# Indexer queries of whole token tiles loaded one tile ahead in a fused two-block transformer kernel

## The chip, the cores and the metric

The kernel runs on one NeuronCore of a Trainium2 chip. That core has five engines with an instruction queue each: TensorE (PE, matrix products), VectorE (DVE), ScalarE (ACT), GpSimd (POOL) and SyncE (SP, which here does nothing but issue DMAs). Every queue is worked off in order: an instruction that waits holds back all that stand behind it. Sixteen DMA engines move data between the chip's main memory and the on-chip memory. The metric is the device time of one execution in microseconds; the kernel before takes 2626.92 us (median of three runs, 2626.12 to 2632.38).

## The reference

Two transformer blocks run one after the other on 1024 tokens of width 1024, in float32. The first (dilated attention, spatial gating, feed-forward) is not touched. The second is, cut to what matters:

```python
def _dsa_attention(q, k, v, q_idx, k_idx, w_idx):     # per block of 128 queries:
    logits = einsum('bthd,bsd->bths', qib, k_idx) * IDX_DIM ** -0.5    # 8 indexer heads of 64
    score = einsum('bth,bths->bts', wb, relu(logits))
    score = where(causal, score, -inf)
    _, sel = lax.top_k(score, 256)                     # keys that this query may look at
    ...                                                # attention of 8 heads over those keys

def second_block(...):
    q, k, v, qi, ki, wi, cu = split(h @ w_in)          # qi: indexer queries, cu: convolution input
    attn_out = _dsa_attention(rope(q), rope(k), v, rope(qi), rope(ki), wi)
    conv_out = _conformer_conv(cu, ...)                # gated; 31 taps per channel; norm; silu
    x = x + gt1 * (concat(attn_out, conv_out) @ w_out)
    x = x + gt2 * (square(relu(norm(x) @ w_up)) @ w_down)
```

## The kernel before, in words

**Tiling.** The 1024 tokens are two halves of 512, and eight tiles of 128 (tiles 0 to 3 in half 0, 4 to 7 in half 1). Every float32 matrix operand of weight is split in a high and a low part, and a product is three matmuls (lines 147, 148, 149), so the feed-forward networks fill most of TensorE's time.

**What runs beside what.** Attention and convolution of block 2 are a chain of dependent steps with little TensorE work. `flow` weaves such a side chain into a feed-forward network: half 0 of block 2 beside the second half of block 1's network (tiles `fa`, `fa1o`), half 1 beside the first half of block 2's own network (`fb`, `fb0o`). `flow` goes by an estimated clock: every `yield e, d` of a side chain says that it spent `e` us of TensorE and wants to be called again `d` us later (`d` from the table `LT`); between the calls feed-forward steps are written out. A scheduler then orders each engine's instructions by priority and by its own estimate of when buffers come free, so that the order on an engine isn't the order of the source.

**The side chain of one half** (`block2_side`, L1330): `b2_glu` writes the convolution's gated input to main memory (`glu_d`); `b2_conv` (L1066) runs as a chain of its own and, for each of four channel groups j, loads `glu` (L1071, one buffer) and does 31 steps on DVE, of which the first (L1073) waits for that load and the others are L1075; `b2_proj` forms the queries, turns them to one row per feature (L1007 to L1015) and stores them in main memory (`qiT_d` for the indexer, `qT_d` for the attention). Then come the scores: for each tile, `b2_scores` (L1128) loads the indexer queries of four heads (`load_q`, L1109), multiplies them by the keys (`scores_mm`, L1125, tiles `ip`), and per head does a relu on ACT (L1143, tile `ir`, in one of the five buffers of tag `PT`) and a multiply-add on DVE (L1146 and L1148, tile `sc`). `b2_topk` searches each query's 256th score bit by bit on DVE (L1162) and ACT (L1183) and ends in a mask (L1220). `b2_attn` (L1222) loads the attention queries with the same `load_q` (tile `qt`), forms scores (L1125, `sp`), masks and exponentiates (L1240, L1243), transposes (L1268), splits the result (L1270, L1271: `PT`, `PL`) and multiplies by the values (`o`).

**The loads in question.** `load_q` fills a tile `q` of 128 x 2 x 512 in two DMAs of 256 KB (z = 0, 1): 64 rows of main memory, read twice to fill 128 partitions. The tag `q` has two buffers (`QB2`), shared by indexer and attention queries, so the loads of a group of four heads wait until the group two before it has been multiplied. Scores of tiles 0 and 1 need no queries, which leaves 8 such DMAs in half 0 and 16 in half 1, each named `qi` in the trace, beside 32 named `qt`.

Of the kernel before, what the change touches and what calls it, by code (L numbers as in the profile page):

```python
# [10 lines left out]
F32R = mybir.dt.float32r  # L11
# [17 lines left out]
LT = {'att0': 11.236,  # L29
 'bit': 2.0,  # L30
 'conv': 12.0,
 'cvn': 3.332,
 'ex': 18.659,
 'fin': 4.025,
 'mods': 5.62,
 'n4': 6.0,
 'norm': 7.406,
 'qk': 12.0,
 'rope': 3.856,
 'ropeT': 2.236,  # L40
# [8 lines left out]
QB2 = 2  # L49
# [68 lines left out]
def tile_hybrid_two_blocks(ctx, tc, A, out, dbg=None, stop=None):  # L118
# [60 lines left out]
    def split_in(src, hi, lo, name):  # L179

        for t in range(2):
            sl = slice(2 * t, 2 * t + 2)
            raw = ring.tile([128, 2, 512], F32, tag="raw", name=f"{name}_r{t}", bufs=RBUF)
            for k in range(2):
                SP.dma_start(raw[:, k, :], src[2 * t + k])
            split_into(raw, hi[:, sl], lo[:, sl])
# [161 lines left out]
    def T_tiles(n, name):  # L348
        return [tp.tile([128, 4, 512], F32R, tag="T", name=f"{name}{i}") for i in range(n)]
# [82 lines left out]
    for td, o, n in ((tabA_d, 0, LA), (tabB_d, LA, LB)):  # L432
        p = psd.tile([NH, n], F32, tag="s", name=f"tabp{o}")
# [14 lines left out]
    for g2 in range(2):  # L448
        p = psd.tile([128, 4, 128], F32, tag="s", name=f"swp{g2}")
# [279 lines left out]
    for half in range(2):  # L729
# [3 lines left out]
        for f in range(4):  # L733
            p = psd.tile([128, 512], F32, tag="s", name=f"sgp{half}{f}")
# [11 lines left out]
    xu = ctx.enter_context(tc.tile_pool(name="xu", bufs=1, reuse_waits="tile"))  # L746
# [100 lines left out]
    for half in range(2):  # L847
# [3 lines left out]
        for q in range(4):  # L851
            i = 4 * half + q
# [90 lines left out]
    p = psd.tile([128, 4, 32], F32, tag="s", name="cwp")  # L943
# [18 lines left out]
    qiT_d = [dram.tile([2, 128, 512], F32, name=f"qiT_d{i}") for i in range(NT)]  # L962
# [143 lines left out]
            DVE.tensor_tensor(cl[:, j, :], ys[:, j, :], ch[:, j, :].bitcast(F32), op=ALU.subtract)  # L1106
        return ch, cl

    def load_q(d, g, name):  # L1109

        q = xu.tile([128, 2, 512], F32R, tag="q", name=name, bufs=QB2)
        for z in range(2):
            SP.dma_start(q[:, z, :].bitcast(F32), bass.AP(tensor=d.tensor, offset=d.offset + z * 128 * 512 + g * 64 * 512,
                                             ap=[[0, 2], [512, 64], [1, 512]]))
        return q

    def spans(n):

        m = n // -(-n // 512)
        return [(c0, m) for c0 in range(0, n, m)]  # L1120

    def scores_mm(q, j, g, c0, m, name):
        p = psd.tile([128, m], F32, tag="s", name=name)
        for z in range(2):
            PE.matmul(p, q[:, z, 128 * j:128 * j + 128], kT[:, g, c0:c0 + m], start=z == 0, stop=z == 1)  # L1125
        return p

    def b2_scores(i, sc):  # L1128

        n = 128 * (i + 1)  # L1130
        dg = slice(n - 128, n)
        if i < 2:
            if i:
                POOL.memset(sc[:, 0:128], 0.0)
            DVE.tensor_scalar(sc[:, dg], tri, -NEG, None, op0=ALU.mult)
            return
        for h in range(8):
            if h % 4 == 0:
                q = load_q(qiT_d[i], h // 4, f"qi{i}{h}")
            for c0, m in spans(n):  # L1140
                p = scores_mm(q, h % 4, 2, c0, m, f"ip{i}{h}")
                t = xu.tile([128, 512], F32, tag="PT", name=f"ir{i}{h}", bufs=PTB)
                ACT.activation(t[:, :m], p, AF.Relu)  # L1143
                o = sc[:, c0:c0 + m]
                if h == 0:
                    DVE.tensor_scalar(o, t[:, :m], wis[:, i, 0:1], None, op0=ALU.mult)  # L1146
                else:
                    DVE.scalar_tensor_tensor(o, t[:, :m], wis[:, i, h:h + 1], o, op0=ALU.mult, op1=ALU.add)  # L1148
            if h % 2 or n > 512:
                e = n / 512 * (1 if n > 512 else 2)  # L1150
                yield 2 * MM * e, LT["score"] * e / 2
        DVE.scalar_tensor_tensor(sc[:, dg], tri, -1.0e38, sc[:, dg], op0=ALU.mult, op1=ALU.add)
# [160 lines left out]
    def end_ffn1(half, acc):  # L1313

        gpf = grow(A["g_post_ffn"][0], f"gpf{half}")
        hi, lo = T_tiles(2, f"h3h{half}"), T_tiles(2, f"h3l{half}")
        for q in range(4):
            i = 4 * half + q
            a = acc[q]
            x = xtile(f"xf{i}")  # L1320
            SP.dma_start(x, x1_d[i])
            r = rms_r(a, 1e-6, f"po{i}")
            DVE.scalar_tensor_tensor(a, a, r, gpf, op0=ALU.mult, op1=ALU.mult)
            DVE.tensor_tensor(x, x, a, op=ALU.add)
            SP.dma_start(x2_d[i], x)
            if "x2" in dbg:
                SP.dma_start(dbg["x2"][128 * i:128 * i + 128], x)
            yield from norm_T(a, x, rms_r(x, 1e-6, f"n3{i}"), hi, lo, q, 0, f"h3{i}")
        return hi, lo

    def block2_side(half, acc):
        Th, Tl = yield from end_ffn1(half, acc)
        yield from b2_glu(half, Th, Tl)
        conv = yield Spawn(b2_conv(half), CP)
        qs = yield from b2_proj(half, Th, Tl)
        tiles = [4 * half + q for q in range(4)]
        sc = {}

        def scores(p):
            t = tp.tile([128, 2, S], F32, tag="T", name=f"sc{p[0]}")  # L1340
            for e, i in enumerate(p):
                sc[i] = t[:, e, :]
                yield from b2_scores(i, sc[i])

        def rows_of(i):
            return sc[i][:, 0:128 * (i + 1)]

        jk = xu.tile([128, S], BF16, tag="jk", name=f"jk{half}", bufs=1)

        def keep(i):  # L1350
            return b2_topk(f"{i}", jk, [rows_of(i)], [rows_of(i + 1)])

        busy[0] += 1
        if half:
            yield from scores(tiles[0:2])
            ks = [(yield Spawn(keep(4)))]
            yield from scores(tiles[2:4])
            ks.append((yield Spawn(keep(6))))
            busy[0] -= 1
            yield Join(qs)  # L1360
            for u in range(2):
                yield Join(ks[u])
                yield 0, LT["att0"]
                yield from b2_attn([(i, sc[i]) for i in tiles[2 * u:2 * u + 2]])
        else:
            yield from scores(tiles[2:4])
            busy[0] -= 1
            k_ = yield Spawn(keep(2))
            yield from scores(tiles[0:2])
            yield Join(qs)  # L1370
            yield from b2_attn([(i, sc[i]) for i in tiles[0:2]])
            yield Join(k_)
            yield 0, LT["att0"]
            yield from b2_attn([(i, sc[i]) for i in tiles[2:4]])
        cv = yield Join(conv)
        mT = [(None, None), cv]

        def mixed(k, q):
            if k < 4 and mT[0][0] is None:
                mT[0] = (T_tiles(1, f"ath{half}")[0], T_tiles(1, f"atl{half}")[0])  # L1380
                split_in(at2_d[half], *mT[0], f"at2{half}")
            return [t[:, k % 4, 128 * q:128 * q + 128] for t in mT[k // 4]]

        w = A["w_out_2"][0]
        gt1 = grow(gate_d[0], f"gt1{half}")
        ss = [small.tile([128, 2], F32, tag="ss4", name=f"ss4{half}{q}", bufs=4) for q in range(4)]
        for c in range(2):
            cs = slice(512 * c, 512 * c + 512)

            def ev(q, p):  # L1390
                i = 4 * half + q
                x = xu.tile([128, 512], F32, tag="P", name=f"x3p{i}{c}", bufs=PB)
                SP.dma_start(x, x2_d[i][:, cs])
                t = xu.tile([128, 512], F32, tag="PT", name=f"x3t{i}{c}", bufs=PTB)
                DVE.tensor_tensor(t, p, gt1[:, cs], op=ALU.mult)
                DVE.tensor_tensor(x, x, t, op=ALU.add)
                SP.dma_start(x3_d[i][:, cs], x)
                ACT.activation(junk[:, 0:512], x, AF.Square, accum_out=ss[q][:, c:c + 1])
            yield Job(tok_steps(mixed, w, [(512 * c, 512)], 2, f"w2{half}{c}", ev, first=4, two=4))
        hi, lo = T_tiles(2, f"h4h{half}"), T_tiles(2, f"h4l{half}")  # L1400
        yield 0, LT["n4"]
        for q in range(4):
            i = 4 * half + q
            s1 = small.tile([128, 1], F32, tag="ss", name=f"ss5{i}")
            DVE.tensor_tensor(s1, ss[q][:, 0:1], ss[q][:, 1:2], op=ALU.add)
            r = rsqrt_mean(s1, D, 1e-6, f"n4{i}")
            x = xtile(f"x4{i}")
            SP.dma_start(x, x3_d[i])
            yield from norm_T(x, x, r, hi, lo, q, 1, f"h4{i}")
        return hi, lo  # L1410
# [65 lines left out]
    acc, _ = flow(ffn1(0), mods())  # L1476
# [29 lines left out]
```

## Time and profile before

| | |
|---|---|
| median of 3 runs | 2626.92 us |
| profiled execution | 2627.51 us, of which the span of recorded instructions is 2625.7 us |
| mean granted TensorE clock | 0.968 of full speed |
| PE / DVE / ACT / POOL busy | 93% / 57% / 46% / 9% of the span |
| indexer products (L1125, `ip`) | 160 matmuls, 63.6 us busy, 51.2 us of PE idle before them |

The span runs from the first recorded instruction to the last; 1.8 us of the profiled execution lie outside it. A row's idle time is what the engine spent without work just before it, put down to what came last.

### The profile page before, as it was taken

The page shows a single profiled execution, that of the slowest core. Times are in us where ns is not written, and L with a number is a line of the kernel's source. Part 1 is how long each engine was busy: PE and PEld are TensorE (multiplying, and loading weights), DVE is VectorE, ACT ScalarE, POOL GpSimd, SP SyncE. Part 2 cuts the span into 40 slices and gives each one's busy share as a digit, 9 for nine tenths or more (in the row PEclk, how much of TensorE's full clock was granted, in tenths as well). Part 3 has the DMA queues.
Part 4 walks back from the last instruction along what each step waited for, and adds up shares of the span by engine and source line. Part 5 has one row for each costly group of instructions (what it writes and reads, how often), then busy time and mean ns, then how long its engine had stood idle before and what let it go on. Part 6 is the DMA issues. An engine that isn't in the chain of part 4 may idle for free.

```text
span 2625.7 us, 32724 instructions
## 1 busy us (share of the span) xinstructions
PE 2448.8 (93%) x12024; PEld 2001.5 (76%) x12024; DVE 1497.4 (57%) x2755; ACT 1216.5 (46%) x2160; POOL 242.4 (9%) x356
## 2 busy tenths in 40 slices
PE   8999999999999999679999999878889999799997
PEld 8867777778788787457888878667678887688886
DVE  3356444476654468367443257799997554533436
ACT  4345554453333443255545373366664443533332
POOL 1034311100000000000000000123200000100002
PEclk9999999999999999689999999989899999899999
DMA  6412114589976666345558657522222225633332
GB/s 180 121 44 64 42 37 118 172 298 320 295 257 194 223 206 220 125 132 179 167 164 271 195 161 212 168 90 80 65 84 80 86 69 160 229 96 96 97 96 72
DMA packets 330784, 391.64 MB, mean 149 GB/s; under 512 B 42273, under 2 KB 227889, under 8 KB 330624
## 3 DMA queue, kind: packets, MB, share of 16 engines
q1 hardware_dynamic: 327216, 385.11, 47.1%
q10 hardware_dynamic: 3408, 4.46, 0.5%
q8 instruction: 94, 1.54, 0.2%
q14 instruction: 66, 0.54, 0.1%
HBM read 312.44 MB, written 80.73 MB: 150 GB/s over the span
## 4 chain that ended last, share of the span: by engine, by line
PE 58%; DVE 14%; DMA 12%; issue 10%; ACT 3%; POOL 2%; SPq 1%; POOLq 0%; DVEq 0%; ACTq 0%
DVE y L1075 4%; DMA qi<-qiT_d 4%; PE fa_p L147 3%; PE fa_p L149 3%; PE fa_p L148 3%; PE fb_p L147 3%; PE fb_p L148 3%; PE fb_p L149 3%; PE oT L685 2%; PE fa0o_p L148 2%; PE fa0o_p L149 2%; PE fa0o_p L147 2%; PE fb1o_p L148 2%; PE fb1o_p L149 2%; PE fb1o_p L147 2%
## 5 line engine op out<-in xcount | busy, mean ns | idle before, releaser
L147 PE MATMUL fb_p<-h4h,fb_w_h 128*128 128x512 f32 x512 | 205.9, 403 | 12.6 <-ACT h4h L841 8.2
L147 PE MATMUL fa_p<-h2h,fa_w_h 128*128 128x512 f32 x512 | 205.1, 401 | 0.7 <-DVE fa_a L795 0.7
L149 PE MATMUL fa_p<-h2h,fa_w_l 128*128 128x512 f32 x512 | 203.9, 398 | 1.8 <-DMA fa_w_l<-fa_w_d 1.8
L148 PE MATMUL fa_p<-h2l,fa_w_h 128*128 128x512 f32 x512 | 204.8, 400 | 0.0
L148 PE MATMUL fb_p<-h4l,fb_w_h 128*128 128x512 f32 x512 | 204.5, 400 | 0.0
L149 PE MATMUL fb_p<-h4h,fb_w_l 128*128 128x512 f32 x512 | 203.5, 398 | 0.0
L1075 DVE SCALAR_TENSOR_TENSOR y<-glu,cw,y 128x512 f32<-128x512 f32 x240 | 193.8, 807 | 4.5
L176 ACT CAST fb_w_h<-fb_w_r 128x1024 fp32r<-128x1024 f32 x64 | 67.2, 1050 | 154.2 <-PE fb1o_p L149 74.1
L147 PEld LDWEIGHTS fb_p<-h4h,fb_w_h 128*128 128x128 f32 x512 | 97.9, 191 | 33.9 <-ACT h4h L841 8.6
L1183 ACT ACTIVATE junk<-sc,cand 128x768 bf16<-128x768 f32 (+2 forms) x93 | 86.8, 934 | 66.7 <-DVE cand L1181 64.7
L147 PEld LDWEIGHTS fa_p<-h2h,fa_w_h 128*128 128x128 f32 x512 | 97.1, 190 | 23.1 <-issue 1.1
L149 PEld LDWEIGHTS fa_p<-h2h,fa_w_l 128*128 128x128 f32 x512 | 96.9, 189 | 22.3 <-DMA fa_w_l<-fa_w_d 2.2
L148 PEld LDWEIGHTS fb_p<-h4l,fb_w_h 128*128 128x128 f32 x512 | 97.7, 191 | 21.0 <-DVE h4l L842 0.4
L148 PEld LDWEIGHTS fa_p<-h2l,fa_w_h 128*128 128x128 f32 x512 | 97.1, 190 | 21.4 <-issue 0.9
L149 PEld LDWEIGHTS fb_p<-h4h,fb_w_l 128*128 128x128 f32 x512 | 97.5, 191 | 20.1
L177 DVE TENSOR_TENSOR fb_w_l<-fb_w_r,fb_w_h 128x1024 fp32r<-128x1024 f32 x53 | 64.8, 1223 | 83.6 <-ACT fb_w_h L176 78.9
L1125 PE MATMUL ip<-kT,qi 128*128 128x384 f32 (+3 forms) x160 | 63.6, 429 | 51.2 <-DMA qi<-qiT_d 39.5
L1271 DVE TENSOR_TENSOR PL<-pt,PT 128x512 fp32r<-128x512 f32 (+1 forms) x80 | 50.6, 635 | 70.5 <-ACT PT L1270 70.5
L176 ACT CAST fa_w_h<-fa_w_r 128x1024 fp32r<-128x1024 f32 x32 | 33.7, 1054 | 118.4 <-PE fa0o_p L149 77.8
L1125 PEld LDWEIGHTS ip<-kT,qi 128*128 128x128 f32 x160 | 35.2, 226 | 65.2 <-DMA qi<-qiT_d 39.0
L1162 DVE TENSOR_SCALAR_CACHE_REDUCE jk<-sc,cand 128x640 bf16<-128x640 f32 (+2 forms) x93 | 81.4, 876 | 1.9
L177 DVE TENSOR_TENSOR fb1o_w_l<-fb1o_w_r,fb1o_w_h 128x1024 fp32r<-128x1024 f32 x28 | 34.3, 1225 | 83.9 <-ACT fb1o_w_h L176 83.9
(1511 smaller groups left out, 7103.1 us busy)
## 6 DMA issues: line engine op xcount, KB each, us to landing
fa_w_r<-in_w_ff_dram SPq DMA_DIRECT2D x64, 512.0 KB
fb_w_r<-in_w_up_dram SPq DMA_DIRECT2D x64, 512.0 KB
ada_w<-in_w_ada_dram SPq DMA_DIRECT2D x48, 512.0 KB
fa_w_d<-fa_w_l SPq DMA_DIRECT2D x32, 512.0 KB
fa0o_w_r<-in_w_ff_dram SPq DMA_DIRECT2D x32, 512.0 KB
fa0o_w_d<-fa0o_w_l SPq DMA_DIRECT2D x32, 512.0 KB
fa_w_l<-fa_w_d SPq DMA_DIRECT2D x32, 512.0 KB
fa1o_w_r<-in_w_ff_dram SPq DMA_DIRECT2D x32, 512.0 KB
```

The costliest lines, as they stand in the source:

```text
L147: PE.matmul(out_, lh, rh, start=first, stop=False)
L148: PE.matmul(out_, lh, rl, start=False, stop=False)
L149: PE.matmul(out_, ll, rh, start=False, stop=last)
L176: ACT.copy(hi, raw)
L177: eng.tensor_tensor(lo, raw, hi.bitcast(F32), op=ALU.subtract)
L685: PE.matmul(o, v, P[:, m, e, :], start=q == 0 and m == 0, stop=q == 7 and m == 1)
L1075: DVE.scalar_tensor_tensor(y, glu[:, k:k + 512], cw[:, j, k:k + 1], y, op0=ALU.mult, op1=ALU.add)
L1125: PE.matmul(p, q[:, z, 128 * j:128 * j + 128], kT[:, g, c0:c0 + m], start=z == 0, stop=z == 1)
L1162: DVE.tensor_scalar(jk[:, :ss[e].shape[-1]], ss[e], thr, 0.0, op0=op, op1=ALU.add, accum_out=cnt[:, e:e + 1])
L1183: ACT.activation(junk[:, :ss[e].shape[-1]], ss[e], AF.Sign, bias=cand[:, e:e + 1].bitcast(F32), accum_out=cnt[:, e:e + 1])
L1271: DVE.tensor_tensor(tl[:, :kk], pt[:, :kk], th[:, :kk].bitcast(F32), op=ALU.subtract)
```

## The change

`load_q` can now fill a tile that it is given. A new `ahead(i)` issues all four DMAs of tile i: for an even tile into two buffers of tag `q`, for an odd tile into one tile of tag `T` (the pool `tp`, eight buffers of 128 x 4 x 512 that otherwise hold feature-major activations and the scores). Tiles 2, 3 (half 0) and 4, 5 (half 1) are loaded before the first score of their pair, followed by a wait of 6 us of `flow`'s clock; tile 6 is loaded after the scores of tile 4, tile 7 after those of tile 5. Number, size and source of the DMAs, and all arithmetic, stay as they are.

```diff
+ 'ql': 6.0,
...
-    def load_q(d, g, name):
-
-        q = xu.tile([128, 2, 512], F32R, tag="q", name=name, bufs=QB2)
+    def load_q(d, g, name, q=None):
+
+        if q is None:
+            q = xu.tile([128, 2, 512], F32R, tag="q", name=name, bufs=QB2)
...
+    qi_of = {}
+
+    def ahead(i):
+        if i % 2:
+            t = T_tiles(1, f"qi{i}_")[0].rearrange("p (g z) t -> p g z t", z=2)
+            qi_of[i] = [load_q(qiT_d[i], g, None, t[:, g]) for g in range(2)]
+        else:
+            qi_of[i] = [load_q(qiT_d[i], g, f"qi{i}{g}") for g in range(2)]
...
+        qs = qi_of.pop(i)
         for h in range(8):
-            if h % 4 == 0:
-                q = load_q(qiT_d[i], h // 4, f"qi{i}{h}")
+            q = qs[h // 4]
...
+                if i > 1 and p[0] in (2, 4) and not e:
+                    ahead(i)
+                    ahead(i + 1)
+                    yield 0, LT["ql"]
                 yield from b2_scores(i, sc[i])
+                if i in (4, 5):
+                    ahead(i + 2)
```

The order on the engines changes with it, since the scheduler places everything anew. Three places follow. In the rows, a name like `qt10_9774` is the tile `qt`, here of tile 1, group 0, with a running number that differs between the two kernels; `x2` means two such rows; line numbers of the changed kernel are 1, 2 or 13 higher here.

SP in half 0, where the last `glu` load of that half (`glu03`) stands among the attention queries `qt` of tiles 0 and 1. Before:

```order
L1113 DMA qt00_9511<-qT_d0_5190 128x1x512
L1113 DMA qt01_9623<-qT_d0_5190 128x1x512
L1015 DMA qT_d3_5193<-qo30_9453 128x512
L162 DMA fa1_8_w_l_9735<-fa0_8_w_d_5734 128x1024
L157 DMA fa1_10_w_r_9904<-in_w_ff1_dram 128x8x128
L1015 DMA qT_d3_5193<-qo31_9456 128x512
L1113 DMA qt01_9623<-qT_d0_5190 128x1x512
L1113 DMA qt10_9774<-qT_d1_5191 128x1x512 x2
L1071 DMA glu03_10063<-glu_d3_5179 128x542
```

The same place on SP now:

```order
L1115 DMA qt00_9528<-qT_d0_5190 128x1x512 x2
L163 DMA fa1_8_w_l_9695<-fa0_8_w_d_5734 128x1024
L158 DMA fa1_10_w_r_9846<-in_w_ff1_dram 128x8x128
L1115 DMA qt01_9657<-qT_d0_5190 128x1x512 x2
L1072 DMA glu03_10044<-glu_d3_5179 128x542
L163 DMA fa1_9_w_l_9767<-fa0_9_w_d_5777 128x1024
L1115 DMA qt10_9816<-qT_d1_5191 128x1x512
L158 DMA fa1o40_w0_r_9940<-in_w_ff2_dram 128x2x512
L1115 DMA qt10_9816<-qT_d1_5191 128x1x512
```

`glu03` stood behind the two loads `qt10` of tile 1 and now stands ahead of them.

SP in half 1, around the last `glu` load (`glu13`); `qi44` is the second group of tile 4, `qi50` the first of tile 5. Before:

```order
L1113 DMA qi44_14263<-qiT_d4_5202 128x1x512
L157 DMA fb0o01_w2_r_14495<-in_w_down_2_dram 128x2x512
L157 DMA fb0_7_w_r_14612<-in_w_up_2_dram 128x8x128
L1071 DMA glu13_14950<-glu_d3_5179 128x542
L1015 DMA qT_d4_5194<-qo40_14234 128x512
L1015 DMA qT_d4_5194<-qo41_14237 128x512
L1113 DMA qi50_14387<-qiT_d5_5203 128x1x512
L157 DMA fb0_8_w_r_14726<-in_w_up_2_dram 128x8x128
L1113 DMA qi50_14387<-qiT_d5_5203 128x1x512
```

The same place now; `qi5_0` is the one tile that holds all of tile 5, and the first of its four loads stands one row above these:

```order
L158 DMA fb0o01_w2_r_14432<-in_w_down_2_dram 128x2x512
L1115 DMA qi5_0_14167<-qiT_d5_5203 128x1x512 x3
L158 DMA fb0_7_w_r_14526<-in_w_up_2_dram 128x8x128
L1072 DMA glu13_14938<-glu_d3_5179 128x542
L1016 DMA qT_d4_5194<-qo40_14211 128x512
L158 DMA fb0_8_w_r_14617<-in_w_up_2_dram 128x8x128
L1016 DMA qT_d4_5194<-qo41_14214 128x512
L1115 DMA qi7_0_14631<-qiT_d7_5205 128x1x512
L1016 DMA qT_d5_5195<-qo50_14257 128x512
L1016 DMA qT_d5_5195<-qo51_14260 128x512
L1115 DMA qi7_0_14631<-qiT_d7_5205 128x1x512 x3
L1115 DMA qi60_14445<-qiT_d6_5204 128x1x512
```

`glu13` stood ahead of every load of tile 5 and now stands behind all four; and the four loads of tile 7 stand ahead of the first of tile 6.

DVE at the same moment, where the convolution's first step on `glu13` meets the first scores of half 1 (`sc4`). Before:

```order
L1146 TENSOR_SCALAR sc4_14161<-ir40_14174,wis_5189 128x320
L973 TENSOR_TENSOR q11_13940<-rope7_14149,ropf7_14150 128x8x16
L1148 SCALAR_TENSOR_TENSOR sc4_14161<-ir41_14196,wis_5189,sc4_14161 128x320
L1075 SCALAR_TENSOR_TENSOR y1_13550<-glu12_14430,cw_5163,y1_13550 128x512
L1148 SCALAR_TENSOR_TENSOR sc4_14161<-ir41_14202,wis_5189,sc4_14161 128x320
L1148 SCALAR_TENSOR_TENSOR sc4_14161<-ir42_14214,wis_5189,sc4_14161 128x320
L1075 SCALAR_TENSOR_TENSOR y1_13550<-glu12_14430,cw_5163,y1_13550 128x512
L1148 SCALAR_TENSOR_TENSOR sc4_14161<-ir42_14220,wis_5189,sc4_14161 128x320
L1014 TENSOR_TENSOR qo41_14237<-qp4_14229,qo40_14234 128x512
L1148 SCALAR_TENSOR_TENSOR sc4_14161<-ir43_14243,wis_5189,sc4_14161 128x320
L1073 TENSOR_SCALAR y1_13550<-glu13_14950,cw_5163,cb_5170 128x512
```

The same place on DVE now:

```order
L1076 SCALAR_TENSOR_TENSOR y1_13549<-glu12_14412,cw_5163,y1_13549 128x512
L974 TENSOR_TENSOR q11_13939<-rope7_14148,ropf7_14149 128x8x16
L1074 TENSOR_SCALAR y1_13549<-glu13_14938,cw_5163,cb_5170 128x512
L1076 SCALAR_TENSOR_TENSOR y1_13549<-glu13_14938,cw_5163,y1_13549 128x512
L1015 TENSOR_TENSOR qo41_14214<-qp4_14206,qo40_14211 128x512
L1159 TENSOR_SCALAR sc4_14160<-ir40_14232,wis_5189 128x320
L1076 SCALAR_TENSOR_TENSOR y1_13549<-glu13_14938,cw_5163,y1_13549 128x512
L1159 TENSOR_SCALAR sc4_14160<-ir40_14238,wis_5189 128x320
```

The step that waits for `glu13` stood behind seven of tile 4's score steps and now stands ahead of the first.

On PE the order of the side chain's own steps stays; what shifts is how many feed-forward matmuls of 512 columns stand ahead of each. Ahead of half 0's first `ip` there are 18 more than before, ahead of tile 0's first `o` 6 more, ahead of tile 1's second group 24 more; in half 1, 28 more ahead of tile 4's first `ip`, 45 more ahead of the third head's `sp` of tile 4, 30 more ahead of tile 7's first `sp`, and as many as before ahead of the output projection, where the feed-forward network has been used up.

## Rows read from the trace of the kernel before

**Rows 1.** Page: busy time by engine; the chain that ended last, by engine.
```profile
PE 2448.8 (93%) x12024; PEld 2001.5 (76%) x12024; DVE 1497.4 (57%) x2755; ACT 1216.5 (46%) x2160; POOL 242.4 (9%) x356
PE 58%; DVE 14%; DMA 12%; issue 10%; ACT 3%; POOL 2%; SPq 1%; POOLq 0%; DVEq 0%; ACTq 0%
```

**Rows 2.** Page, costliest groups: busy, mean ns, idle before and what ended it.
```profile
L1125 PE MATMUL ip<-kT,qi 128*128 128x384 f32 (+3 forms) x160 | 63.6, 429 | 51.2 <-DMA qi<-qiT_d 39.5
```

**Rows 3.** Windows: length, busy PE, PEld, DVE, ACT, POOL; PE clock, DMA share, GB/s.
```profile
1040.00:1100.00 60.00, 33.99 (x110) 25.56 (x110) 26.32 (x57) 13.66 (x25) 0.00 (x0) 0.70 0.40 131
1100.00:1122.00 22.00, 16.85 (x64) 13.13 (x62) 8.96 (x37) 11.95 (x27) 0.00 (x0) 0.82 0.38 125
1122.00:1140.00 18.00, 1.33 (x6) 1.09 (x5) 1.74 (x7) 0.26 (x2) 0.00 (x0) 0.58 0.36 111
1680.00:1740.00 60.00, 42.83 (x168) 33.87 (x167) 45.02 (x80) 24.07 (x49) 10.76 (x4) 0.86 0.40 129
1740.00:2000.00 260.00, 225.58 (x960) 179.12 (x958) 249.50 (x539) 162.68 (x275) 47.70 (x22) 0.93 0.25 78
2000.00:2200.00 200.00, 199.93 (x1096) 167.74 (x1095) 108.64 (x202) 91.44 (x149) 2.76 (x4) 1.00 0.26 82
```

**Rows 4.** Waits between 1040 and 1140 us: total, times, longest.
```profile
PE ip L1125 <- DMA qi<-qiT_d: 26.0, 8, 5.7
DVE y L1073 <- DMA glu<-glu_d: 17.5, 1, 17.5
PE o L148 <- DVE PL L1271: 12.8, 1, 12.8
```

**Rows 5.** DMA issues: KB each.
```profile
qi<-qiT_d SPq DMA_DIRECT2D x24, 256.0 KB
```

**Rows 6.** Windows of 2 us in which only query loads run.
```profile
1050.00:1052.00 2.00, 1.61 (x5) 1.00 (x4) 0.00 (x0) 0.00 (x0) 0.00 (x0) 0.50 0.13 49
1078.00:1080.00 2.00, 2.00 (x8) 1.61 (x7) 0.06 (x1) 0.00 (x0) 0.00 (x0) 0.50 0.13 51
1704.00:1706.00 2.00, 0.00 (x0) 0.00 (x0) 0.00 (x0) 0.00 (x0) 0.00 (x0) 1.00 0.13 49
```

**Rows 7.** SP's timeline: start, duration of the issue, DMA.
```profile
1112.45 9.93 SPq L1113 DMA_DIRECT2D qt<-qT_d  x3
1122.43 5.11 SPq L1071 DMA_DIRECT2D glu<-glu_d  x1
```

**Rows 8.** Chain of waits in half 0: start, length, what.
```profile
1122.43 15.80 DMA glu<-glu_d
...
1138.72 0.43 DVE PL L1271
```

**Rows 9.** DVE's timeline: start, duration; idle before and its end in brackets.
```profile
1138.26 0.55 DVE L1073 TENSOR_SCALAR y<-glu,cw,cb 128x512 f32<-128x512 f32 x1 [17.54 <-DMA glu<-glu_d]
...
1139.06 0.74 DVE L1075 SCALAR_TENSOR_TENSOR y<-glu,cw,y 128x512 f32<-128x512 f32 x1
```

**Rows 10.** A window of feed-forward matmuls alone.
```profile
2300.00:2320.00 20.00, 20.00 (x90) 16.53 (x90) 4.10 (x4) 8.34 (x12) 0.00 (x0) 1.00 0.38 106
```

**Rows 11.** Chain of waits in half 1.
```profile
1673.35 16.02 DMA qi<-qiT_d
```

**Rows 12.** SP's timeline in half 1.
```profile
1686.06 0.86 SPq L1071 DMA_DIRECT2D glu<-glu_d  x1
```

**Rows 13.** DVE's timeline in half 1: first score, first step on `glu13`, last mask.
```profile
1681.98 0.37 DVE L1146 TENSOR_SCALAR sc<-ir,wis 128x320 f32<-128x320 f32 x1
...
1692.71 1.63 DVE L1073 TENSOR_SCALAR y<-glu,cw,cb 128x512 f32<-128x512 f32 x1 [5.16 <-DMA glu<-glu_d]
...
1991.31 0.69 DVE L1220 TENSOR_SCALAR sc<-sc 128x1024 f32<-128x1024 f32 x1
```

**Rows 14.** PE's timeline, a wait for feed-forward weights behind the `qt` loads.
```profile
1198.46 0.50 PE L149 MATMUL fa_p<-h2h,fa_w_l 128*128 128x512 f32 x1 [1.79 <-DMA fa_w_l<-fa_w_d]
```

## The prediction

> **What bounds the kernel now.** I read the shares first: TensorE is busy for 93% of the span, 177 us of it idle, and the chain that ended last is made up of PE for 58%, DVE for 14% and DMA for 12% [rows 1]. So a gain must come out of PE's idle time, at a place where nothing else takes it up. Among the costliest groups one is plainly the change's target: the indexer products have 51.2 us of PE idle before them, 39.5 us of it ended by a `qi` load [rows 2]. Next the windows, to see where that idle lies. In half 0, from 1040 to 1140 us, PE is busy for 33.99 + 16.85 + 1.33 us, so it stands for 48 us of 100. In half 1 it loses 17 us from 1680 to 1740, and 34 us more to 2000, where DVE is the busy one (249.50 of 260 us). From 2000 to 2200 PE is full [rows 3]. Of the 48 us the waits give 26.0 to `qi`, and 12.8 to a `PL` that DVE delivered late, because DVE itself stood 17.5 us for a `glu` load [rows 4].
>
> Then I asked what a load takes. It is 256 KB [rows 5]. Wherever only such loads run, the DMA share is 0.13, two engines of sixteen, and 49 to 51 GB/s pass, though several loads have been issued by then [rows 6]: all of them go through the same two engines, one after the other, 262,144 bytes at 50 GB/s = 5.2 us each. Three windows don't prove that for every moment, but the sizes fit where a wait can be counted: `glu` was issued at 1122.43, right behind three such loads [rows 7], and landed 15.8 us later [rows 8], three times 5.2. So these two engines are a queue of their own. The change takes no byte and no load out of it; it changes who stands in front of whom.
>
> The Trainium skill (DMA: Bandwidth & Descriptors, section Bandwidth, Measured) has 64 KB to 128 partitions in 0.95 us and 1 MB in 6.15; by these a 256 KB load would be some 2 us (an estimate), four in a row 8 us, and a load ahead would nearly always be in time. The rows of 0.13 speak against it, and the same page says why (section on the semaphore's increment by 16, How many engines): a DMA takes as many engines, up to 16, as divide the slowest dimension of both sides; here the source's is 2. By the page's rate the half 1 term below would be nearly nothing.
>
> **The change part by part.** The sum is made against the profiled execution's 2627.5 us, which is 0.6 above the median.
>
> *Removed and added instructions:* none but the loads' new places; the same 24 DMAs, the same matmuls. The 6 us in `flow`'s table cost no engine anything by themselves; they put more feed-forward matmuls ahead of the scores (18 of them in half 0). One such matmul is 20 / 90 = 0.22 us at full clock [rows 10].
>
> *Half 0, a gain.* The `qi` loads are back to back on the two engines already, apart from short transfers between, so the last indexer product comes at most 2 or 3 us earlier, however early the loads are issued. PE's waits for `qi` mostly move: matmuls that fill them are missing later. What counts is `glu03`. It stood behind the two loads of `qt10` and now stands ahead of them: 2 x 5.2 = 10.4 us, and 2 us from the start, so it lands at about 1126 instead of 1138.3. Before, `PL` came one DVE step after it [rows 8, 9]; now four steps of the convolution at 0.74 us and three short ones stand between, 5 us. `PL` at 1131 instead of 1138.7, 7.7 us earlier, and PE has by then 6 feed-forward matmuls more behind it, 1.3 us. Together 9 us less PE idle. It is a true gain only if PE isn't stopped by the next thing. That is the weights: behind the next `qt` loads one came 1.8 us late [rows 14]. Bounds: 0, if such waits take it all, and 14, if all 24 matmuls that stand further ahead by tile 1's second group (5.3 us) fill idle time on top of 7.7 and 1. I take 9, the row of 12.8 us less the part that the longer queue on DVE gives back.
>
> *Half 1, a loss.* Here the same queue works the other way. `glu13` was issued at 1686.06 [rows 12], and DVE stood 5.2 us for it at 1687.5, with seven score steps done before [rows 13]. Now its load is behind all four loads of tile 5, and its step on DVE ahead of every score. The second group of tile 4 had landed 16.0 us after 1673.35 [rows 11], at 1689.4; four loads are 21 us more, and two weight transfers, a sixteenth of 512 KB on each engine at 25 GB/s, 1.3 us each: `glu13` lands at about 1713. DVE reaches that step at about 1682, where the first score stood [rows 13], and stands 31 us. Queued behind it are all scores of tiles 4 and 5; behind these, through the five buffers of the relu's results, ACT; and behind ACT the `ip` matmuls, with the feed-forward matmuls between them. What this doesn't cost: before, DVE idles 60 - 45.0 = 15 us from 1680 to 1740, for loads one at a time [rows 3]. Once `glu13` is there, the loads of tiles 4 and 5 are too, and DVE has some 38 us of scores and convolution without a stop, to 1751. Tile 6's loads, now behind the four of tile 7, land then: 1713 + 21 + 2 x 5.2, with stores and a weight between, is 1747 to 1753. So that second inversion is covered by the first; without the first, it would cost as much by itself. Net, DVE is 31 - 15 = 16 us behind.
>
> How much of 16 us reaches the end? DVE idles only 10.5 us of the next 260 [rows 3]; I let it regain 4, so the last mask, at 1991.3 before [rows 13], is 12 us late. PE meanwhile has more feed-forward matmuls to do ahead of the same points: 30 x 0.22 = 6.6 us at tile 7's first `sp`. That much lateness is filled with work that would have come later, and the rest, 12 - 6.6 = 5 us, stays, since PE is full from 2000 on and the network is used up at the output projection in both. Bounds: -5 (a gain), if DVE makes up the 16 and the extra matmuls fill PE's 34 idle us; 16, if nothing is made up. I take 5, since the row of 10.5 us is near to the upper end.
>
> *Sum:* 2627.5 - 9 + 5 = 2623.5 for the profiled execution, 2623 against the median: 4 us faster, within what a measurement of this kernel can tell from no change, 0.3% or 7.9 us.
>
> **The rivals.**
>
> 1. *Half 1 costs nothing*: `glu13` is late, but DVE's backlog drains before tile 6's masks are asked for. For it: PE idles 34 us between 1740 and 2000, and the masks are hundreds of us after the scores. Against: DVE is 96% busy there. 2627 - 9 - 2 = 2616; with half 1's gain of 5, 2613.
>
> 2. *The waits vanish as meant*: 39.5 us of [rows 2] go, 2627 - 39.5 = 2588. It needs idle DMA engines before the scores; the share of 0.13 says that the two are never done early. By the skill's rate above this would be the likely case.
>
> 3. *Half 0's gain is eaten* by weights behind the loads [rows 14], and half 1 is free: 2625 to 2628.
>
> 4. *Slower: the stand of DVE in half 1 reaches the end.* Place: DVE's first step on `glu13`, with tiles 4 and 5 behind it, in a stretch where DVE then works to 2000 without a break. Price: 16 us, with half 0 giving only 4 back: 2639. It decides from the point where DVE regains under 4 of its 16 us and PE runs out of matmuls written ahead of the masks. For it: 10.5 us of slack in 260. Against: 45 more matmuls (10 us) stand ahead of the third head of tile 4, just where the first mask is late.
>
> **How the numbers follow.** My forecast's case, both terms near their values (2615 to 2631), 0.42; half 1 free 0.18; waits vanish 0.04; gain eaten 0.10; slower 0.26. Of the forecast's 0.42, 0.10 lies under 2619 and 0.02 over 2634.8 when the terms' errors add up. Faster by over 0.3%: 0.10 + 0.18 + 0.04 = 0.32. Slower: 0.26 + 0.02 = 0.28. Same: 0.40. The range leaves out the vanishing waits and the tails: 2606 (half 0 at 14, half 1 at -5, is 2608) to 2642 (half 0 at 0 or 1, half 1 at 16). The likeliest case's own range is 2615 to 2631.
>
> **What would show it.** Half 0: `glu03` lands near 1126 and the 12.8 us before `o` shrink to about 5; PE busy from 1040 to 1140 rises from 52 to about 60 us. Half 1: one DVE wait for `glu` of about 30 us starting near 1680 (all times less the 9 us gained), scores of tiles 4 and 5 without waits, DVE's windows over 95% to 2010. Loads still at a share of 0.13 when alone. I am wrong if a window of loads alone shows more than 0.13, if `glu13` is waited for under 10 us, or if PE's full stretch begins earlier than 1990.

## The result, and the profile after

The changed kernel takes 2652.55 us (median of 4 runs, 2649.86 to 2656.26); the kernel before, beside it, 2628.03. The ratio is 1.0093, 95% interval 1.0077 to 1.0108: 24.5 us slower, outside the range that was given. The profiled execution took 2649.86 us, with a span of 2648.1.

The page after, in the order of [rows 1] and [rows 2]: busy time by engine, the chain that ended last, the indexer products.

```profile
PE 2436.6 (92%) x12024; PEld 1995.8 (75%) x12024; DVE 1496.3 (57%) x2754; ACT 1216.1 (46%) x2160; POOL 246.2 (9%) x357
...
PE 66%; DVE 13%; DMA 8%; issue 5%; ACT 4%; SPq 2%; POOL 2%; POOLq 0%; ACTq 0%; DVEq 0%
...
L1127 PE MATMUL ip<-kT,qi 128*128 128x384 f32 (+3 forms) x160 | 60.8, 404 | 75.6 <-ACT ir L1156 46.0
```

PE's idle time before the indexer products grew from 51.2 to 75.6 us, and it is no longer a `qi` load that ends most of it, but ACT's relu. The stretches of [rows 3] again (length, busy PE, PEld, DVE, ACT, POOL, then TensorE's granted clock, DMA share and GB/s), with the 40 us before 1680 added:

```profile
1040.00:1100.00 60.00, 29.57 (x111) 22.83 (x111) 25.97 (x55) 13.48 (x23) 0.21 (x1) 0.74 0.44 143
1100.00:1122.00 22.00, 15.38 (x58) 11.92 (x57) 8.81 (x24) 10.17 (x21) 0.00 (x0) 0.77 0.39 118
1122.00:1140.00 18.00, 10.82 (x44) 8.26 (x44) 10.57 (x34) 6.49 (x17) 0.00 (x0) 0.81 0.37 121
1640.00:1680.00 40.00, 29.27 (x139) 23.35 (x137) 31.34 (x49) 8.58 (x12) 7.47 (x3) 0.91 0.40 138
1680.00:1740.00 60.00, 18.84 (x72) 15.07 (x73) 18.81 (x30) 12.33 (x25) 5.18 (x2) 0.61 0.32 104
1740.00:2000.00 260.00, 220.62 (x938) 177.32 (x937) 241.50 (x531) 166.55 (x289) 58.25 (x25) 0.93 0.23 72
2000.00:2200.00 200.00, 197.30 (x1071) 164.84 (x1070) 127.56 (x235) 92.15 (x153) 1.84 (x3) 1.00 0.25 77
```

Half 0 gained: PE is busy 55.8 us from 1040 to 1140 against 52.2, and 552.0 against 545.9 from 1040 to 1640. Half 1 lost far more: from 1640 to 1740 PE is busy 48.1 us against 80.8, and DVE 50.1 against 82.5. Both lose 32 to 33 us there, and neither has a stretch up to 2200 that makes up for it. TensorE's mean granted clock from 1680 to 1740 is 0.61 of full speed instead of 0.86; over the whole execution it is 0.965 instead of 0.968.

Waits of half 0, 1040 to 1140 us, beside [rows 4] (total, times, longest):

```profile
ACT ir L1156 <- DMA qT_d<-qo: 16.9, 2, 16.5
...
PE ip L1127 <- DMA qi<-qiT_d: 14.0, 4, 7.4
...
DVE y L1074 <- DMA glu<-glu_d: 8.7, 1, 8.7
...
PE o L148 <- ACT PT L1283: 7.1, 1, 7.1
```

The wait for `glu03` fell from 17.5 to 8.7 us and PE's before `o` from 12.8 to 7.1. In exchange a relu on ACT now stands 16.5 us at once for the *store* of an attention query; before, such a wait took 7.1 us in all of this stretch.

Half 1 on DVE (start, duration; idle before it and what ended that), beside [rows 13]:

```profile
1701.76 0.55 DVE L1074 TENSOR_SCALAR y<-glu,cw,cb 128x512 f32<-128x512 f32 x1 [29.80 <-DMA glu<-glu_d]
...
1735.95 0.55 DVE L1161 SCALAR_TENSOR_TENSOR sc<-ir,wis,sc 128x320 f32<-128x320 f32 x1 [18.98 <-ACT ir L1156]
...
2021.24 0.69 DVE L1233 TENSOR_SCALAR sc<-sc 128x1024 f32<-128x1024 f32 x1
```

DVE stands twice: 29.8 us for `glu13`, and, 15 us of work later, 19.0 us for a relu. The last mask comes at 2021.2 instead of 1991.3. ACT's timeline says what the relu waits for:

```profile
1682.92 1.04 ACT L177 CAST fb0o_w_h<-fb0o_w_r 128x1024 fp32r<-128x1024 f32 x1 [17.97 <-DMA fb0o_w_r<-in_w_down_dram]
...
1735.48 0.77 ACT L1156 ACTIVATE ir<-ip 128x320 f32<-128x320 f32 x2 [19.76 <-DMA qT_d<-qo]
```

Again the store of a query. A query on its way to main memory (`qo`, L1010) and the relu's result (`ir`, L1155) take their tiles from the same five buffers of tag `PT`; the relu can't write until the store has read its buffer. SP's timeline (start, duration of the issue, DMA) shows where that store stood:

```profile
1672.39 12.12 SPq L1115 DMA_DIRECT2D qi<-qiT_d  x3
1684.62 5.36 SPq L158 DMA_DIRECT2D fb_w_r<-in_w_up_dram  x1
1690.07 5.35 SPq L1072 DMA_DIRECT2D glu<-glu_d  x1
...
1707.70 13.03 SPq L1115 DMA_DIRECT2D qi<-qiT_d  x4
1720.83 4.98 SPq L1016 DMA_DIRECT2D qT_d<-qo  x1
```

Three loads of tile 7 and one of tile 6, issued ahead, stand right before it. Issuing the four holds SP for 13.0 us; the store is issued at 1720.83. The chain of waits of that stretch (start, length, what) adds how long each transfer then took:

```profile
1667.35 15.19 DMA fb0o_w_r<-in_w_down_dram
...
1690.07 11.66 DMA glu<-glu_d
...
1720.83 14.57 DMA qT_d<-qo
```

A weight, `glu13` and the store of an attention query: none of the three is an indexer query, each takes 12 to 15 us, and each was issued behind `qi` loads. Where only query loads run, the share is still 0.13, as in [rows 6]:

```profile
1718.00:1720.00 2.00, 0.00 (x0) 0.00 (x0) 0.00 (x0) 0.00 (x0) 0.00 (x0) 1.00 0.13 51
```

In these 2 us no engine did anything.

### The profile page after: what moved, and what is told of

It reads as the page before. It is cut to its first block, busy times and chain, and to the rows that moved or that the text cites. A ratio compares the mean times of both kernels' runs of the same rounds, so it can differ in the third digit from the quotient of the medians.

```text
span 2648.1 us, 32719 instructions
## 1 busy us (share of the span) xinstructions
PE 2436.6 (92%) x12024; PEld 1995.8 (75%) x12024; DVE 1496.3 (57%) x2754; ACT 1216.1 (46%) x2160; POOL 246.2 (9%) x357
## 4 chain that ended last, share of the span: by engine, by line
PE 66%; DVE 13%; DMA 8%; issue 5%; ACT 4%; SPq 2%; POOL 2%; POOLq 0%; ACTq 0%; DVEq 0%
PE fa_p L150 4%; PE fa_p L149 4%; PE fa_p L148 4%; PE fb_p L148 3%; PE fb_p L149 3%; PE fb_p L150 3%; PE oT L686 2%; PE fa0o_p L149 2%; PE fa0o_p L150 2%; PE fa0o_p L148 2%; DVE y L1076 2%; DVE jk L1175 2%; PE fa1o_p L148 2%; PE fb1o_p L149 2%; PE fa1o_p L150 2%
## 5 line engine op out<-in xcount | busy, mean ns | idle before, releaser
L1127 PE MATMUL ip<-kT,qi 128*128 128x384 f32 (+3 forms) x160 | 60.8, 404 | 75.6 <-ACT ir L1156 46.0
L149 PEld LDWEIGHTS fb_p<-h4l,fb_w_h 128*128 128x128 f32 x512 | 97.7, 191 | 20.5 <-issue 0.2
L1161 DVE SCALAR_TENSOR_TENSOR sc<-ir,wis,sc 128x384 f32<-128x384 f32 (+3 forms) x70 | 51.1, 743 | 51.2 <-ACT ir L1156 50.5
```

Of the source, the lines that this page charges most:

```text
L149: PE.matmul(out_, lh, rl, start=False, stop=False)
```

## The experiments

Times are ratios to the kernel before on the same chip, with their 95% interval; medians of before were 2624.6 to 2626.9 us. Line numbers shift by up to 13 between the kernels.

**The two halves apart.** `e1_half0` loads only tiles 2 and 3 ahead, `e2_half1` only tiles 4 to 7; the other half loads at its use, as before.

```diff
-                if i > 1 and p[0] in (2, 4) and not e:
+                if i > 1 and p[0] == 2 and not e:      # e1; e2 has == 4
...
-                if i in (4, 5):                         # e1 only
-                    ahead(i + 2)
```

> Only tiles 2 and 3 are loaded ahead; half 1 loads as before. Theory: half 0 by itself gains, since the last gate input of half 0 is loaded ahead of two attention-query loads and DVE stands less for it; PE is 6 us busier up to 1640 us in the changed kernel, so 6 us faster than before (ratio 0.9977), glu of half 0 waited for some 6 us instead of 17.5. Rival (the gain of half 0 is eaten later, or the whole change is harmful in both halves): ratio 1.000 or more.

> Only tiles 4 to 7 are loaded ahead; half 0 loads as before. Theory: all of the loss lies here, 22 us of longer span plus the 6 that half 0 gave back, so 28 us slower than before (ratio 1.0107), with DVE standing about 30 us for the last gate input and about 19 us for a relu on ACT that waits for an attention-query store. Rival (the loss comes from both halves): 10 to 20 us slower.

`e1_half0`: 0.9963 (0.9952 to 0.9975), 9.7 us faster. `e2_half1`: 1.0133 (1.0120 to 1.0146), 35 us slower. Both are larger than expected (6 and 28 us), but they add up to the whole, -9.7 + 35 = 25 against 24.5. So the halves can be judged apart: half 0's gain is real and of the size forecast, and half 1 costs seven times its term.

**Tiles 6 and 7 at their use.** `e3_no67` keeps the changed order for tiles 2 to 5 and drops the last two lines of the change.

> Tiles 2 to 5 ahead, tiles 6 and 7 loaded at their use as before. On SP the stores of the attention queries of tiles 4 and 5 then stand ahead of all loads of tiles 6 and 7. Theory (the loss of half 1 is the sum of two stands of DVE, 30 us for the gate input behind tile 5's loads and 19 us for a store behind tile 7's loads, less the 15 us that DVE idled before): the second stand goes, the first stays; 19 us faster than the changed kernel, ratio to before about 1.001 to 1.003. Rival (the gate input alone makes the loss, the second stand is covered): as slow as the changed kernel, ratio 1.008 to 1.009.

1.0036 (1.0024 to 1.0048), 2636.07 us: against the whole change 1.0093 - 1.0036 = 0.57%, 15 us. Loading 6 and 7 ahead is 15 of the 34 us by which `e1` and the whole change differ. DVE's first stand is still there, and the long second one is gone:

```profile
1705.48 0.55 DVE L1074 TENSOR_SCALAR y<-glu,cw,cb 128x512 f32<-128x512 f32 x1 [31.17 <-DMA glu<-glu_d]
...
1724.01 0.55 DVE L1164 SCALAR_TENSOR_TENSOR sc<-ir,wis,sc 128x320 f32<-128x320 f32 x1 [3.28 <-ACT ir L1159]
...
2007.08 0.69 DVE L1236 TENSOR_SCALAR sc<-sc 128x1024 f32<-128x1024 f32 x1
```

The last mask is at 2007.1, 14 us earlier than with the whole change. One stand, one half of the loss, so far.

**Every load cut in two.** `e4_spread` is the kernel *before* with each 256 KB load issued as two DMAs of 64 partitions, so that the slowest dimension of the source is 64 rows and not the repetition of 2.

```diff
-            SP.dma_start(q[:, z, :]..., bass.AP(..., ap=[[0, 2], [512, 64], [1, 512]]))
+            for c in range(2):
+                SP.dma_start(q[64 * c:64 * c + 64, z, :]..., bass.AP(..., ap=[[512, 64], [1, 512]]))
```

> The kernel before, with each query load cut in two of 64 partitions, so that no dimension of size 2 is the slowest: twice as many loads (qi and qt), the same bytes. Theory (each load runs on two engines because of that dimension, and these two engines are the queue in which everything waits): the DMA share while only such loads run rises from 0.13 to several tenths, loads of 128 KB take about 0.5 us each, the waits of PE for qi and qt fall from 46 us to under 10 and DVE's for the gate input of half 0 from 17.5 to under 4; PE idle of 48 us between 1040 and 1140 falls to about 12, that of half 1 by some 10: 40 to 50 us faster, ratio 0.981 to 0.985. Rival (the loads are slow for another reason, or SP's issuing becomes the limit with twice as many): share stays at 0.13, ratio 1.00 or above.

0.9719 (0.9706 to 0.9731), 74 us faster, more than expected. Its windows, against the first and third of [rows 3]:

```profile
1040.00:1100.00 60.00, 55.56 (x259) 43.83 (x258) 43.32 (x118) 36.07 (x71) 0.00 (x0) 1.00 0.85 259
1122.00:1140.00 18.00, 18.00 (x90) 14.90 (x89) 18.00 (x46) 8.24 (x16) 1.02 (x1) 1.00 0.62 178
```

PE is busy 55.6 us of 60 instead of 34.0 and the DMA share is 0.85 instead of 0.40: the loads were short of DMA engines, not of time ahead. Other DMAs run in these windows too, so 0.85 isn't the share of the query loads alone. `load_q` serves the attention queries as well, so the 74 us contain their 32 loads; how much each kind gives was not separated.

**Taking the first victim away.** If the stands add up, a buffer of its own for `glu13`, which lets its load be issued early, should take some 15 us off. It was tried on the kernel before, on `e3` and on the whole change.

```diff
-            glu = xu.tile([128, 542], F32, tag="glu", ...)
+            glu = xu.tile([128, 542], F32, tag="glu" if (half, j) != (1, 3) else "gluB", ...)
```

> Control: the kernel before, with a buffer of its own for the last gate input of half 1 (glu13), whose load then stands ahead of all query loads of that half on SP. Theory (the load costs little here, since before it stood behind one group of tile 4 only and DVE waited 5.2 us): 0 to 5 us faster, ratio 0.998 to 1.000. Rival (this load's place is worth as much in the kernel before as in the changed one): 15 to 20 us faster.

> As e3 (tiles 2 to 5 ahead, 6 and 7 at their use), with glu13 in a buffer of its own and so ahead of tile 5's four loads. Theory (in e3 the 30 us stand of DVE for glu13 is the loss of half 1): DVE's wait for glu in half 1 under 3 us, and all of half 1's loss gone; ratio to before 0.995 to 0.998, 15 to 22 us faster than e3. Rival (the loss comes from loading tile 5 in one piece ahead, whatever DVE waits for): within 5 us of e3, ratio 1.002 or more.

> The changed kernel with glu13 in a buffer of its own. The attention-query stores of tile 5 still stand behind loads of tile 7, and the relus on ACT need the buffers that these stores free. Theory (two stands, each with its own price, that add): the first stand goes, the second of about 19 us stays; ratio to before 1.001 to 1.004, some 15 to 20 us faster than the changed kernel. Rival (the second stand is covered once the first is gone, as DVE then has convolution steps left): ratio 0.995 to 0.998.

`e5_glubuf_before` 0.9986 (0.9978 to 0.9995), `e6_glubuf_no67` 1.0034 (1.0021 to 1.0046), `e7_glubuf_all` 1.0080 (1.0068 to 1.0092). The long wait for `glu13` is gone in all three, yet next to `e3` nothing is won, and the interval of `e7` overlaps that of the whole change (1.0077 to 1.0108). The theory that the stands add up fell. The control `e5` gains 0.14% by itself, some 4 us, which are in `e6` and `e7` too. In `e6`, ACT and then DVE stand at the same time for something else:

```profile
1701.48 0.44 ACT L1159 ACTIVATE ir<-ip 128x320 f32<-128x320 f32 x1 [18.77 <-DMA qT_d<-qo]
...
1701.95 0.55 DVE L1164 SCALAR_TENSOR_TENSOR sc<-ir,wis,sc 128x320 f32<-128x320 f32 x1 [17.46 <-ACT ir L1159]
```

The store of a query behind tile 5's loads had been late all along, under the cover of the longer stand. (These rows are those of the fastest of `e6`'s six executions, 2629.8 us; the slowest took 2639.4.) In `e7` such stores hold ACT's relus for 34.4 us between 1640 and 1780, in three waits.

**Taking the second victim away.** Half 1's `qo` go into tiles of tag `T`, so that a late store holds no relu; alone (`e11`) and with the buffer for `glu13`.

```diff
-                o = xu.tile([128, 512], F32R, tag="PT", name=f"{nm}o{i}{z}", bufs=PTB)
+                if half and nm == "q":
+                    if q % 2 == 0 and z == 0:
+                        tt = T_tiles(1, f"qoT{i}")[0]
+                    o = tt[:, 2 * (q % 2) + z, :]
+                else:
+                    o = xu.tile([128, 512], F32R, tag="PT", ...)
```

> Control: the kernel before with glu13 in a buffer of its own (as e5), and half 1's rotated attention queries (qo) in two tiles of tag T and not in the five buffers that the relus use, so that no relu waits for an attention-query store. Theory: little changes without loading ahead, since these waits were short: ratio 0.995 to 0.999. Rival (buffers alone are worth as much with the loads as before): 0.993 or less.

> As e6 (tiles 2 to 5 ahead, glu13 in its own buffer), and also qo of half 1 off the relus' buffers. Theory formed after e6 (glu13 and the attention-query stores of tile 4 stand behind the same four loads of tile 5, so the two stands of DVE lie over each other, 31 us for the one, 17.5 us via ACT's relu for the other, and taking one away only shows the other): with both gone DVE stands under 13 us between 1660 and 1720, and 8 to 15 us of e6 come back: ratio 0.997 to 1.001. Rival (a third one is covered by these two: the weight tile that ACT splits, which stood 13 to 18 us behind the same loads, ahead of the relus): still 1.002 to 1.005.

> As e3 (tiles 2 to 5 ahead) with qo of half 1 off the relus' buffers, glu13 behind tile 5's loads as in e3. Theory (stands that lie over each other): the 31 us for glu13 stay and the time is that of e3 within 4 us, ratio 1.002 to 1.005. Rival (the stores alone make the loss): 0.997 to 1.000.

> The changed kernel with both: glu13 in its own buffer, qo of half 1 off the relus' buffers. Theory: both stands of DVE are gone, also that behind tile 7's loads, since no relu waits for a store any more; ratio 0.996 to 1.001, 20 us or more faster than the changed kernel. Rival (loading tile 7 ahead of tile 6 costs by itself): 1.004 or more, over 8 us slower than e10.

`e9_both_before` (both edits on the kernel before) 0.9984 (0.9974 to 0.9994); `e10_both_no67` 1.0003 (0.9993 to 1.0012); `e11_qo_no67` 1.0027 (1.0016 to 1.0038); `e12_both_all` 1.0050 (1.0037 to 1.0063). From `e3` the buffer for `glu13` alone gives nothing measurable and the tiles for `qo` alone no more than their interval, but both together 1.0036 - 1.0003 = 0.33%, 9 us. That is what two stands that lie over each other would give. The times alone bear it weakly: the control `e9` shows that both edits give the kernel before 0.16%, 4 us, so only some 5 of the 9 us are left, about what the intervals can tell apart. The rows bear it better. DVE's longest stand at this place is 31.2 us in `e3`, 17.5 in `e6` for the store and 30.1 in `e11`, where the wait for `glu13` stands again as it was:

```profile
1708.16 0.55 DVE L1079 TENSOR_SCALAR y<-glu,cw,cb 128x512 f32<-128x512 f32 x1 [30.14 <-DMA glu<-glu_d]
```

And `e10`, with both gone, is still 1.0003 - 0.9963 = 0.4%, 10 us, above `e1`; some 14 if the 4 us of the control are taken off. Its third victim is a feed-forward weight. First ACT's timeline, then DVE's:

```profile
1682.82 1.04 ACT L177 CAST fb0o_w_h<-fb0o_w_r 128x1024 fp32r<-128x1024 f32 x1 [12.98 <-DMA fb0o_w_r<-in_w_down_dram]
...
1706.23 1.04 ACT L177 CAST fb_w_h<-fb_w_r 128x1024 fp32r<-128x1024 f32 x1 [13.87 <-DMA fb_w_r<-in_w_up_dram]
```

```profile
1707.65 3.36 DVE L1169 SCALAR_TENSOR_TENSOR sc<-ir,wis,sc 128x320 f32<-128x320 f32 x3 [13.18 <-ACT ir L1164]
```

ACT stands in order too: a relu behind a cast whose weight is late makes DVE wait for a `qi` that landed long ago. `e12` has the same once more, 20.5 us, behind the loads of tiles 6 and 7. So its rival came true: without either stand, loading tiles 6 and 7 ahead still costs 1.0050 - 1.0003 = 0.47%, 12 us.

**The changed order with loads that are cut in two.** `e8_spread_all` is the whole change with the edit of `e4`, nothing else.

> The changed kernel with each query load cut in two of 64 partitions, as in e4. Theory (what made loading ahead harmful was the queue of two engines; with loads of half a microsecond nothing stands behind them, and the waits for queries that loading ahead could remove are 3 us): same as e4 within 5 us, ratio to before 0.970 to 0.974, no DVE wait for glu over 3 us. Rival (the reordering itself, more feed-forward matmuls or query loads ahead of stores, is what hurts): 15 to 25 us slower than e4, ratio 0.978 or more.

0.9705 (0.9692 to 0.9717), 2548.07 us, the fastest of all. Against `e4` (0.9706 to 0.9731) the intervals overlap: loads of whole tiles ahead, which cost 24.5 us as they were, now cost nothing measurable. The scores of half 1 come some 60 us earlier in this kernel, so its rows are read from 1570 on. SP's timeline has the last load of the convolution behind all of half 1's query loads, further back than in the changed kernel:

```profile
1636.74 4.31 SPq L1116 DMA_DIRECT2D qi<-qiT_d  x4
1644.26 5.07 SPq L1116 DMA_DIRECT2D qi<-qiT_d  x8
1651.52 0.47 SPq L1072 DMA_DIRECT2D glu<-glu_d  x1
```

Eight of these loads, half the size each, are issued in 5.1 us. The waits from 1590 to 1660, and the window of 60 us in which the scores of half 1 begin:

```profile
ACT ir L1158 <- DMA qT_d<-qo: 2.1, 1, 2.1
...
DVE y L1074 <- DMA glu<-glu_d: 0.8, 1, 0.8
```

```profile
1600.00:1660.00 60.00, 54.63 (x258) 45.38 (x257) 48.77 (x74) 31.20 (x61) 18.63 (x8) 0.97 0.66 188
```

The two victims of the changed kernel wait 0.8 and 2.1 us; PE is busy 54.6 us of 60, where the changed kernel has 18.8 in its worst 60. That shows the cause: loads that go through two DMA engines, placed ahead of other transfers. The scheduler places every instruction anew in `e8` as well, so it isn't the changed kernel's order to the letter; but the loads of whole tiles ahead, the tiles that they take, the 6 us in `flow`'s clock and a `glu13` behind the loads are all there, and cost nothing measurable once the loads are cut in two.

## Why the prediction was wrong

**What bounds the kernel: right.** The loads share two engines, one after the other; 0.13 stands again, and cutting the loads in two lifts the share to 0.85 and takes 74 us away. The Trainium skill's rule in DMA: Bandwidth & Descriptors (section on the semaphore's increment by 16, How many engines), that the slowest dimensions of both sides set how many engines a DMA takes, agrees with the 0.13, two of sixteen; the 0.85 of `e4`, whose slowest dimension is 64, fits it, though other DMAs run there too.

**Half 0, 9 us: right in size** (`e1`: 9.7), and the path that was forecast stands in the rows: `glu03` came earlier, PE's wait before `o` fell from 12.8 to 7.1 us, and PE is busy 10.82 us instead of 1.33 from 1122 to 1140. But `glu03` came at 1129.3, not 1126, and PE's busy time from 1040 to 1140 rose to 55.8 and not to 60: from 1040 to 1100 PE lost 4.4 us, where the new wait for a query's store is. The text counted the `qi` loads that move ahead, and `glu03` behind `qt`, but not the stores `qT_d` among them. By 1640 PE is 6.1 us busier and has 60 matmuls more behind it (2553 against 2493 from 1040 on), at a mean granted clock of 0.96 instead of 0.94, for which the sum had no term. No run moved `glu03` alone, so how the 9.7 us divide isn't shown, and part of the agreement may be luck.

**Half 1, the first stand: right.** "DVE reaches that step at about 1682 [...] and stands 31 us"; it stood 29.8, and `glu13` was there at 1701.8, where 1713 less the 9 us gained had been said.

**Half 1, what follows: the step that failed.** The prediction put it: "Once `glu13` is there, the loads of tiles 4 and 5 are too, and DVE has some 38 us of scores and convolution without a stop, to 1751 [...] So that second inversion is covered by the first". DVE had 15 us and then stood 19.0 more. The loads were there; the relu's buffer was not, since tile 6's store stood behind three loads of tile 7 and one of its own tile on SP. Those loads were looked at as something that makes tile 6's own scores late, and by that measure they are covered. That each of them also delays every other transfer issued after it was written down for `glu13` alone, though the same holds for stores and weights; the rows of the order showed two stores `qT_d` among the loads of tile 7, and the one that the relu waited for, tile 6's first, is the next on SP behind the last of those rows.

In the terms of the sum, the changed kernel is best set beside `e1`, which has half 0's gain too and half 1 as before. DVE was to be 31 - 15 = 16 us behind. By 1740 it is 83.8 - 50.1 = 34 us behind (busy time from 1640, in `e1` and now), the second stand making up most of the difference. It was to regain 4. In `e1` the last mask comes at 1977.8:

```profile
1977.82 0.69 DVE L1236 TENSOR_SCALAR sc<-sc 128x1024 f32<-128x1024 f32 x1
```

That is 43.4 us ahead of the changed kernel's 2021.24, with the same 313 us of DVE work from 1640 to the mask in both: DVE regained nothing and lost some 10 us more. (Beside the kernel before it is 29.9 us late, but there half 0's gain has been taken off already.)

Last, 6.6 us were to be filled with matmuls that stand further ahead. Up to 1740 nothing was filled: PE loses as much as DVE there, 32.7 us beside the kernel before. PE's instructions are in order too, and the `ip` matmuls, waiting for relus, stood between those matmuls and PE. Later something was: of the 43.4 us, 36 reach the end (spans of 2648.1 and 2612.1), so some 7 do not, near to the 6.6 (2 us of both numbers lie between the two executions before half 0 begins); that it's these matmuls isn't shown. A late mask isn't lost time by itself: in `e8` it comes 14.7 us after that of `e4` (1925.8 and 1911.1), and `e8` is no slower.

So the term is not 5 but about 34 us (`e2`: 35; the whole change less `e1`: 1.0093 - 0.9963 = 1.3%, 34 us), and what it had wrong is the second stand, which it took to be covered, and the 4 us to be regained.

**The rivals.** The fourth, that the stand of DVE in half 1 reaches the end, was the right one in sign and place, at 0.26; its price of 16 us was taken from the same sum and lacked the same second stand. Its condition, that DVE regains under 4 us, is what the rows show. The forecast that windows of DVE would be over 95% to 2010 failed (241.50 of 260 us, 93%), and so did that of scores of tiles 4 and 5 without waits. The signs under "I am wrong if" all guard against a change that does better than forecast; none looks for a second stand. The first rival fell with the 35 us of `e2`, the second with the idle time before `ip`, which grew from 51.2 to 75.6 us. The third, weights behind loads, took nothing of half 0's gain that shows in the time of `e1`, but weights are the third victim of half 1 in `e10`.

**What stays open.** Between `e10` and `e1` lie 10 us, or some 14 by the control. The rows show two waits for weights of 13 and 14 us on ACT, but no run took these away alone.

## What to carry to other kernels

Before moving a load ahead, ask how many DMA engines it takes, and list every transfer issued behind its new place, stores and weights too, with the buffers that each holds: the load may be in time and still make the others late. Where a DMA source repeats rows, a small repetition as its slowest dimension can make a narrow queue, as it did here; cutting it by partitions was worth 74 us, while the reordering cost 24.5. And stands that share one cause can lie over each other: taking one victim away shows the next, so it is the cause that must be tested.

## What the runs showed of the hardware

A DMA's issue itself can hold SP. A lone `qi` load takes about 0.55 us to issue (0.64 at 1654.77 in the changed kernel), but once several are on the way it is some 3 to 5 us each on average, and 7.2 at the longest: 12.12 for three, 13.03 for four, 23.12 for five in half 0 (1056.48). Then the DMAs behind them on SP are not only slow but not yet issued. In `e8`, with twice as many loads of half the size, no `qi` load took over 1.3 us to issue. This is one way in which loads on two of the sixteen engines delay other transfers. The prediction had not counted on it, though [rows 7] already has 9.93 us for three loads; no run here separates the time on SP from the time in the two engines.
